# A transformer block in one kernel: when the second feed-forward products load residuals, join kept sums and fetch their chunks

## The chip, the core and the metric

The kernel runs on one core of one Trainium2 chip. The metric is device time in microseconds (us), as the median of the runs shown. One further execution was taken with the hardware profiler; its page and trace are read below. Engines are called PE (TensorE, matmuls), PEld (its weight loads), DVE (VectorE), ACT (ScalarE), POOL (GpSimd) and SP (SyncE, which here issues nearly all DMAs). L1509 is line 1509 of the kernel.

## The reference, cut to what matters

One layer over 2048 latent tokens of width 1024: token mixing (attention and a gated MLP), then the channel part. Only the last lines matter here:

```
h2 = modulate(x, norm2_g, sh2, sc2)
x = x + g2 * sq_relu_mlp(h2, w_ff1, w_ff2)     # square(relu(h2 @ w_ff1)) @ w_ff2
```

x on the right is the residual (2048 x 1024), g2 a row of 1024 factors, w_ff1 is 1024 x 4096 and w_ff2 4096 x 1024. Everything is fp32.

## The kernel before, in words

**Arithmetic.** Every fp32 operand is split into a high part h, rounded to the type that PE multiplies, and a remainder l, also in that type. A product is three matmuls: h by h (L1418), h by l (L1419), l by h (L1420), all added in one PSUM bank. The large products are cut into two by two blocks, and seven block products are formed instead of eight (a Strassen scheme); some sums of products are kept aside and used in two results.

**Feed-forward.** ffn (L1594) handles the tokens in two blocks of 1024. For each block ff1 (L1479) makes the activations in 16 groups and writes, ready for the second products, seven combined operands to DRAM (ao_d), as ff1_group does at L1446 to L1476. The weights w_ff2, combined in the same way, lie in wo_d (w2o_d in the trace), written once during the first ff1. Then ff2 (L1513) forms the second products of the block. So ff2(0), ff1(1) and ff2(1) follow each other at the end of the kernel.

**ff2.** It takes the products in the order 0, 1, 5, 6, 4, 2, 3 (L1563), each in eight chunks of 256 rows of the inner dimension: 56 steps (L1566). A chunk is 512 KB of ao_d and 512 KB of wo_d. ff2_chunk (L1502) loads each with one DMA on SP (L1507), rounds it on ACT (L1508, 128 x 1024 at a time) and subtracts on DVE for the remainder (L1509). A chunk takes four buffers of the tag b4, which has 12. Loads are made two chunks ahead: step n emits the load of chunk n + 2 (L1568). A step has four groups of six matmuls, one group per 128 tokens, each group in its own PSUM bank (128 x 512).

At the end of a product (step with c = 7) take (L1544) handles the four banks:
- products 0, 5, 6: ACT copies the bank to an f2 buffer, as kept sum u2 (0, then 5) or u3 (6) (L1548, L1555);
- product 1: the result leaves, then ACT copies the kept u2 back into the bank (L1551), on which product 5 goes on;
- products 4, 2: DVE adds the kept sum and the bank (L1558), and the result leaves; 2 goes on in the banks of 4, so in 2 the kept sum is u2 with the earlier parts in PSUM;
- product 3: the result leaves.

leave (L1535) multiplies by g2 on DVE, adds the residual xs on DVE, and puts the store to the output on a list (late, L1542). The traces give the line of the small helper, L1521, for all these DVE operations. The list is worked off in the next step, after the loads of that step (L1569). residual (L1526) loads the four xs tiles (256 KB each, L1530); it is called in the last chunk of products 1, 4, 2 and 3 (L1578). xs, kept sums, results and the side work's tiles all come from the tag f2, which has 16 buffers of 128 x 512.

**Side work.** In every step of ff2(0) one piece of side work is emitted (L1587): first the row g2 (mod_part, 12 steps, L321), then h_ops (L1328), which prepares the operands of ff1(1) in four rounds of five steps: load and scale x (L1267), transposes on PE and copies out on ACT (L1282, L1289), sums, and splits into high part and remainder (L1255, L1263 and L1264). Those operands fill all 35 buffers of the tag hb until ff1(1) ends; its products run in the order 0, 5, 1, 6, 4, 3, 2, and hb holds the operands of 6, 4, 3, 2 and a part of 1. hb is free during ff2(1).

**Order.** The tile framework sets semaphores and places each engine's instructions by a plan of its own; the sequence in the code is its priority, not its result. order (L1689) ties first writes to tiles of one tag to the code's sequence, and holds SP to it within ff2 (self.loads, L1592, L1704). ACT, DVE and PE are free to be reordered by the plan. At run time each engine works its queue strictly in that order.

Of the kernel before, what the change touches and what calls it, by code (L numbers as in the profile page):

```python
# [11 lines left out]
F32R = mybir.dt.float32r  # L12
I32 = mybir.dt.int32
AF = mybir.ActivationFunctionType
ALU = mybir.AluOpType
# [4 lines left out]
P = 128  # L20
# [10 lines left out]
TB = 512  # L31
NB = SEQ // TB
TT = TB // P
# [11 lines left out]
NCH = NG // 2  # L45
# [6 lines left out]
def f32(ap):  # L52
    return ap.bitcast(F32)
# [17 lines left out]
class Kern:  # L71
# [1427 lines left out]
            for _ in more:  # L1499
                pass  # L1500

    def ff2_chunk(self, blk, p, c):  # L1502
        nc = self.nc
        out = []
        for src in (self.ao_d[blk][p][c], self.wo_d[p][c]):
            l, h = self.sb("b4", [2, TB], F32R), self.sb("b4", [2, TB], F32R)
            nc.sync.dma_start(f32(l), src.rearrange("s p c -> p s c"))  # L1507
            nc.scalar.copy(h, f32(l))  # L1508
            nc.vector.tensor_tensor(out=l, in0=f32(l), in1=f32(h), op=ALU.subtract)  # L1509
            out.append((h, l))  # L1510
        return out

    def ff2(self, blk, side):  # L1513
        nc = self.nc
        add, mult = ALU.add, ALU.mult
        ready = self.ready + [self.ff2_chunk(blk, 0, 1)]
        begin = self.here()
        late = []

        def tt(out, in0, in1, op):  # L1520
            nc.vector.tensor_tensor(out=out, in0=in0, in1=in1, op=op)  # L1521

        goes = {1: (0, 0), 4: (1, 1), 2: (0, 1), 3: (1, 0)}
        u2, u3, xs = ([None] * TT for _ in range(3))

        def residual(p):  # L1526
            i, j = goes[p]
            for t in range(TT):
                xs[t] = self.sb("f2", [TB])
                nc.sync.dma_start(  # L1530
                    xs[t],
                    self.x1_d[2 * blk + i][t * P : (t + 1) * P, j * TB : (j + 1) * TB],
                )

        def leave(p, t, src):  # L1535
            i, j = goes[p]
            row = (2 * blk + i) * TB + t * P
            cs = slice(j * TB, (j + 1) * TB)
            c = self.sb("f2", [TB])
            tt(c, src, self.g2b[:, cs], mult)  # L1540
            tt(c, c, xs[t], add)
            late.append(lambda: nc.sync.dma_start(self.out[0, row : row + P, cs], c))  # L1542

        def take(p, t):  # L1544
            ps = banks[p][t]
            if p == 0:
                u2[t] = self.sb("f2", [TB])
                nc.scalar.copy(u2[t], ps)  # L1548
            elif p == 1:
                leave(p, t, ps)  # L1550
                nc.scalar.copy(ps, u2[t])  # L1551
            elif p in (5, 6):
                u = u2 if p == 5 else u3
                u[t] = self.sb("f2", [TB])
                nc.scalar.copy(u[t], ps)  # L1555
            elif p in (4, 2):
                u = u3[t] if p == 4 else u2[t]
                tt(u, u, ps, add)  # L1558
                leave(p, t, u)
            else:  # L1560
                leave(p, t, ps)

        order = (0, 1, 5, 6, 4, 2, 3)  # L1563
        steps = [(p, c) for p in order for c in range(NCH)]
        banks = {}
        for n, (p, c) in enumerate(steps):  # L1566
            if n + 2 < len(steps):
                ready.append(self.ff2_chunk(blk, *steps[n + 2]))  # L1568
            for f in late:  # L1569
                f()  # L1570
            late.clear()
            (ah, al), (wh, wl) = ready.pop(0)
            fresh = p in (0, 4)
            if c == 0 and fresh:
                new = [self.bank([TB]) for _ in range(TT)]
                for other in (0, 1, 5, 6, 3) if p == 0 else (4, 2):
                    banks[other] = new
            if c == NCH - 1 and p in goes:  # L1578
                residual(p)
            for t in range(TT):  # L1580
                tok = slice(t * P, (t + 1) * P)
                a = [(ah[:, s, tok], al[:, s, tok]) for s in range(2)]
                b = [(wh[:, s], wl[:, s]) for s in range(2)]
                self.product(banks[p][t], a, b, fresh and c == 0)
                if c == NCH - 1:
                    take(p, t)
            next(side, None)  # L1587
        for f in late:
            f()
        for _ in side:  # L1590
            pass
        self.loads.append(range(begin, self.here()))  # L1592

    def ffn(self, h, w, w1, late):  # L1594
        for _ in w1:
            pass
        next(late)
        next(late)
        self.ff1(0, h, self.w2_ops, w, late)
        self.g2b = self.sb("g1", [D])  # L1600
        h = self.operand_lists()
        side = chain(self.mod_part(lambda: self.sb("f2", [TB]), ("g2",)), self.h_ops(1, h))
        self.ff2(0, side)
        self.ff1(1, h, lambda g: iter(()))
        self.ff2(1, iter(()))
# [449 lines left out]
```

## Time and profile before

| | |
|---|---|
| runs | 3120.96, 3128.94, 3130.93 us; median 3128.94 |
| profiled execution, first to last instruction (span) | 3128.1 us; the page gives no other time of it |
| PE busy | 3011.9 us, 96% |
| PEld, DVE, ACT, POOL busy | 2261.8, 2070.7, 1459.0, 688.3 us |
| chain that ended last, PE's share | 79%; DMA 8%, DVE 6%, ACT 3% |
| mean granted clock of PE | 0.982 |
| ff2(0), ff1(1), ff2(1) | from about 2167, 2499 and 2807 us of the span |

How to read the lines below. A group line has: line, engine, operation, out<-in by tile names without buffer numbers, shapes, xcount, then busy us, mean ns of one, idle us of the engine just before them and who ended it. A timeline line has start us, duration us, engine, line, what, and in brackets the idle time before and its releaser. A wait line has who waited, for whom, total us, times, longest us. Durations of neighbouring matmuls overlap, since they are pipelined; their pace is read from their starts. In tile names b is the tag b4, f is f2 (or f8, f9), g is the row g2.

### The profile page before, as it was taken

How to read it: one execution, taken by the hardware profiler on the slowest of the kernel's cores; microseconds unless marked ns; L12 is line 12 of the kernel's file. 1: busy time of each engine (PE TensorE's matmuls, PEld its weight loads, DVE VectorE, ACT ScalarE, POOL GpSimd, SP SyncE). 2: the span in 40 equal slices, each digit the busy share in tenths (PEclk: the TensorE clock that was granted, in tenths of full speed). 3: DMA queues.
4: the chain of work that ended last, by engine and by line, in shares of the span. 5: the costliest groups of instructions: out<-in, count | busy, mean ns of one | idle time of the engine just before them, and what ended most of it. 6: DMA issues, size and time to landing. Idle time of an engine off the chain costs nothing.

```text
span 3128.1 us, 37962 instructions
## 1 busy us (share of the span) xinstructions
PE 3011.9 (96%) x13508; PEld 2261.8 (72%) x13508; DVE 2070.7 (66%) x2930; ACT 1459.0 (47%) x2290; POOL 688.3 (22%) x506
## 2 busy tenths in 40 slices
PE   7799999988999999999989989999999999999999
PEld 3778788866555555555867878888777788888777
DVE  3767477875887767767664478876665576654445
ACT  4545765563555554545222245444454354444433
POOL 0000000000888888886144200000000000000000
PEclk9899999999999999999999999999999999999999
DMA  7586657654001000004864448888766644445665
GB/s 260 169 271 216 209 188 226 198 170 145 27 31 38 12 7 18 11 8 159 271 217 158 138 150 314 307 301 289 247 218 220 207 144 155 154 161 194 205 214 202
DMA packets 389807, 534.33 MB, mean 171 GB/s; under 512 B 37968, under 2 KB 209104, under 8 KB 389616
## 3 DMA queue, kind: packets, MB, share of 16 engines
q1 hardware_dynamic: 374720, 515.88, 49.7%
q10 hardware_dynamic: 14896, 16.02, 1.5%
q8 instruction: 106, 1.74, 0.2%
q14 instruction: 85, 0.70, 0.1%
HBM read 367.69 MB, written 164.10 MB: 170 GB/s over the span
## 4 chain that ended last, share of the span: by engine, by line
PE 79%; DMA 8%; DVE 6%; ACT 3%; issue 2%; POOL 1%; SPq 1%; ACTq 0%; DVEq 0%; POOLq 0%
PE b L1419 13%; PE b L1420 13%; PE b L1418 13%; PE b L1947 8%; PE b L1914 5%; PE b L1933 4%; PE b L183 4%; PE b L185 4%; PE b L184 4%; PE b L1879 3%; PE a L1418 2%; PE a L1419 2%; PE a L1420 2%; PE b L189 2%; DMA f<-in_w_in 1%
## 5 line engine op out<-in xcount | busy, mean ns | idle before, releaser
L1509 DVE TENSOR_TENSOR b<-b,b 128x1024 fp32r<-128x1024 f32 x224 | 273.0, 1224 | 246.4 <-ACT b L1508 241.8
L1890 DVE TENSOR_REDUCE ts<-b 128x1 f32<-128x512 f32 x512 | 314.9, 682 | 142.2 <-PE b L1879 142.0
L1508 ACT CAST b<-b 128x1024 fp32r<-128x1024 f32 x224 | 234.9, 1052 | 332.5 <-DMA b<-ao_d 298.1
L1419 PE MATMUL b<-b,b 128*128 128x512 f32 x896 | 351.6, 392 | 4.1 <-DVE b L1509 3.5
L1420 PE MATMUL b<-b,b 128*128 128x512 f32 x896 | 349.7, 390 | 0.0
L1418 PE MATMUL b<-b,b 128*128 128x512 f32 x896 | 309.0, 395 | 12.4 <-ACT b L1508 7.6
L1963 POOL TENSOR_TENSOR ac<-ac,p 128x512 f32<-128x512 f32 x216 | 302.2, 1433 | 67.8 <-ACT p L1937 67.2
L1937 ACT ACTIVATE p<-b 128x512 f32<-128x512 f32 x384 | 199.8, 614 | 167.0 <-PE b L1933 157.1
L1963 POOL TENSOR_TENSOR ac<-ac,t 128x512 f32<-128x512 f32 x152 | 217.8, 1460 | 0.0
L1418 PEld LDWEIGHTS b<-b,b 128*128 128x128 f32 x896 | 168.4, 189 | 54.7 <-ACT b L1508 11.9
L1914 PE MATMUL b<-h,h 128*128 128x512 f32 x576 | 200.9, 419 | 1.8 <-DVE ts L1890 1.2
L1419 PEld LDWEIGHTS b<-b,b 128*128 128x128 f32 x896 | 168.9, 188 | 45.4 <-DVE b L1509 10.7
L1420 PEld LDWEIGHTS b<-b,b 128*128 128x128 f32 x896 | 168.7, 188 | 34.6
L1933 PE MATMUL b<-h,h 128*128 128x512 f32 x576 | 180.7, 395 | 0.0
L1947 PE MATMUL b<-p,h 128*64 128x512 f32 x768 | 175.3, 598 | 0.0
L1419 PE MATMUL b<-hb,b 128*128 128x512 f32 x448 | 174.6, 390 | 0.0
L1836 POOL MEMSET t<- 128x512 f32 x16 | 8.4, 527 | 723.0 <-DMA tb_d<-t 699.5
L1418 PE MATMUL b<-hb,b 128*128 128x512 f32 x416 | 162.1, 390 | 0.0
L1420 PE MATMUL b<-hb,b 128*128 128x512 f32 x416 | 161.5, 389 | 0.0
L1428 DVE TENSOR_TENSOR f<-f,b 128x512 f32<-128x512 f32 x160 | 109.3, 683 | 65.9 <-issue 43.2
L1914 PEld LDWEIGHTS b<-h,h 128*128 128x128 f32 x576 | 107.0, 190 | 59.3 <-DVE ts L1890 20.1
L1418 PE MATMUL a<-f,h 128*128 128x384 f32 (+1 forms) x320 | 119.3, 376 | 14.5 <-ACT a L608 8.5
(393 smaller groups left out, 6920.0 us busy)
## 6 DMA issues: line engine op xcount, KB each, us to landing
ao_d<-f SPq DMA_DIRECT2D x224, 256.0 KB
b<-ao_d SPq DMA_DIRECT2D x112, 512.0 KB
b<-w2o_d SPq DMA_DIRECT2D x112, 512.0 KB
f<-in_w_ff SPq DMA_DIRECT2D x48, 1024.0 KB
w2o_d<-f SPq DMA_DIRECT2D x112, 256.0 KB
f<-in_w_in SPq DMA_DIRECT2D x46, 512.0 KB
f<-x_d SPq DMA_DIRECT2D x64, 256.0 KB
m<-p_d SPq DMA_DIRECT2D x20, 512.0 KB
```

What stands on the lines that cost most here:

```text
L183: mm(ps, sh, mh, start=start, stop=False)
L1418: mm(ps, wh, hh, start=start and k == 0, stop=False, skip_group_check=True)
L1419: mm(ps, wh, hl, start=False, stop=False, skip_group_check=True)
L1420: mm(ps, wl, hh, start=False, stop=k == len(w) - 1, skip_group_check=True)
L1508: nc.scalar.copy(h, f32(l))
L1509: nc.vector.tensor_tensor(out=l, in0=f32(l), in1=f32(h), op=ALU.subtract)
L1890: nc.vector.tensor_reduce(out=self.mx[:, t, h, c : c + 1], in_=ps[h], axis=AX.X, op=ALU.max)
L1914: self.nc.tensor.matmul(self.pts[j][h], k.KA[c][self.kv][:, ks], self.qa[h], start=True, stop=False, skip_group_check=True,)
L1933: self.nc.tensor.matmul(s, k.KB[c][self.kv][:, ks], self.qb[h], start=False, stop=True, skip_group_check=True,)
L1937: self.nc.scalar.activation(pt[h], s, AF.Exp)
L1947: nc.tensor.matmul(self.o[h * HD : (h + 1) * HD, :], k.V[c][:, i, self.kv * HD : (self.kv + 1) * HD], pt[h], start=j == 0, stop=j == NKT - 1,)
L1963: nc.gpsimd.tensor_tensor(out=self.acc[e][:, h], in0=old[:, h], in1=pt[h], op=ALU.add)
```

## The change

It touches ff2_chunk, ff2 and one line of ffn.

1. Residuals (xs) are loaded in chunk 5 of products 1, 4, 2, 3 instead of chunk 7.
2. For products 4 and 2 the kept sum is joined to the residual beforehand: carried, emitted in chunk 6, multiplies the kept sum by g2 and adds it to xs. At the end of the product only the bank is multiplied by g2 there.
3. leave emits only the multiplication. The addition of xs is put on the list with the store, and so is emitted in the next step, after the loads of that step.
4. In ff2(1) chunks are fetched four ahead instead of two. Odd chunks are loaded there in four pieces of 256 KB into hb buffers (eight per chunk), with four casts and four subtractions of 128 x 512; even chunks as before into b4.
5. In ff2(0) two empty steps stand between mod_part and h_ops, so that h_ops starts two chunks later.

```
-    def ff2_chunk(self, blk, p, c):
+    def ff2_chunk(self, blk, p, c, apart=False):
...
         for src in (self.ao_d[blk][p][c], self.wo_d[p][c]):
+            if apart:
+                pairs = []
+                for s in range(2):
+                    l, h = self.sb("hb", [TB], F32R), self.sb("hb", [TB], F32R)
+                    nc.sync.dma_start(f32(l), src[s])
+                    nc.scalar.copy(h, f32(l))
+                    nc.vector.tensor_tensor(out=l, in0=f32(l), in1=f32(h), op=ALU.subtract)
+                    pairs.append((h, l))
+                out.append(pairs)
+                continue
...
-        ready = self.ready + [self.ff2_chunk(blk, 0, 1)]
+        ahead = 4 if blk else 2
+        def chunk(n):
+            return self.ff2_chunk(blk, *steps[n], bool(blk) and n % 2 == 1)
+        ready = self.ready + [chunk(n) for n in range(1, ahead)]
...
+        def carried(p):
+            _, cs = place(p)
+            for t in range(TT):
+                u = (u3 if p == 4 else u2)[t]
+                tt(u, u, self.g2b[:, cs], mult)
+                tt(xs[t], xs[t], u, add)
...
         def leave(p, t, src):
...
+            c, x = self.sb("f2", [TB]), xs[t]
             tt(c, src, self.g2b[:, cs], mult)
-            tt(c, c, xs[t], add)
-            late.append(lambda: nc.sync.dma_start(self.out[0, row : row + P, cs], c))
+            def rest():
+                tt(c, c, x, add)
+                lo = row + t * P
+                nc.sync.dma_start(self.out[0, lo : lo + P, cs], c)
+            late.append(rest)
...
-            elif p in (4, 2):
-                u = u3[t] if p == 4 else u2[t]
-                tt(u, u, ps, add)
-                leave(p, t, u)
...
-            if n + 2 < len(steps):
-                ready.append(self.ff2_chunk(blk, *steps[n + 2]))
+            if n + ahead < len(steps):
+                ready.append(chunk(n + ahead))
...
-            if c == NCH - 1 and p in goes:
+            if c == NCH - 3 and p in goes:
                 residual(p)
+            if c == NCH - 2 and p in (4, 2):
+                carried(p)
...
-        side = chain(self.mod_part(lambda: self.sb("f2", [TB]), ("g2",)), self.h_ops(1, h))
+        side = chain(
+            self.mod_part(lambda: self.sb("f2", [TB]), ("g2",)), [None] * 2, self.h_ops(1, h)
+        )
```

More of the change, by code (lines that the diff above doesn't have):

```diff
@@ L1509, in ff2_chunk @@
             nc.vector.tensor_tensor(out=l, in0=f32(l), in1=f32(h), op=ALU.subtract)
-            out.append((h, l))
+            out.append([(h[:, s], l[:, s]) for s in range(2)])
         return out
@@ L1515, in ff2 @@
         add, mult = ALU.add, ALU.mult
-        ready = self.ready + [self.ff2_chunk(blk, 0, 1)]
+        order = (0, 1, 5, 6, 4, 2, 3)
+        steps = [(p, c) for p in order for c in range(NCH)]
+        ahead = 4 if blk else 2
+        def chunk(n):
+            return self.ff2_chunk(blk, *steps[n], bool(blk) and n % 2 == 1)
+        ready = self.ready + [chunk(n) for n in range(1, ahead)]
         begin = self.here()
@@ L1524, in ff2, with place @@
         u2, u3, xs = ([None] * TT for _ in range(3))
+        def place(p):
+            i, j = goes[p]
+            return (2 * blk + i) * TB, slice(j * TB, (j + 1) * TB)
         def residual(p):
@@ L1533, in residual @@
                 )
+        def carried(p):
[4 more added lines that the diff above has]
+                tt(xs[t], xs[t], u, add)
         def leave(p, t, src):
[L1536 to L1539, printed above, removed]
+            row, cs = place(p)
+            c, x = self.sb("f2", [TB]), xs[t]
             tt(c, src, self.g2b[:, cs], mult)
-            tt(c, c, xs[t], add)
-            late.append(lambda: nc.sync.dma_start(self.out[0, row : row + P, cs], c))
+            def rest():
[3 more added lines that the diff above has]
+            late.append(rest)
         def take(p, t):
             ps = banks[p][t]
[L1546 to L1553, printed above, removed]
+            if p in (0, 5, 6):
+                u = u3 if p == 6 else u2
                 u[t] = self.sb("f2", [TB])
                 nc.scalar.copy(u[t], ps)
-            elif p in (4, 2):
-                u = u3[t] if p == 4 else u2[t]
-                tt(u, u, ps, add)
-                leave(p, t, u)
             else:
                 leave(p, t, ps)
-        order = (0, 1, 5, 6, 4, 2, 3)
-        steps = [(p, c) for p in order for c in range(NCH)]
+                if p == 1:
+                    nc.scalar.copy(ps, u2[t])
         banks = {}
         for n, (p, c) in enumerate(steps):
-            if n + 2 < len(steps):
-                ready.append(self.ff2_chunk(blk, *steps[n + 2]))
+            if n + ahead < len(steps):
+                ready.append(chunk(n + ahead))
             for f in late:
@@ L1571, in ff2 @@
             late.clear()
-            (ah, al), (wh, wl) = ready.pop(0)
+            a, b = ready.pop(0)
             fresh = p in (0, 4)
@@ L1577, in ff2 @@
                     banks[other] = new
-            if c == NCH - 1 and p in goes:
+            if c == NCH - 3 and p in goes:
                 residual(p)
+            if c == NCH - 2 and p in (4, 2):
+                carried(p)
             for t in range(TT):
                 tok = slice(t * P, (t + 1) * P)
-                a = [(ah[:, s, tok], al[:, s, tok]) for s in range(2)]
-                b = [(wh[:, s], wl[:, s]) for s in range(2)]
-                self.product(banks[p][t], a, b, fresh and c == 0)
+                at = [tuple(x[:, tok] for x in pair) for pair in a]
+                self.product(banks[p][t], at, b, fresh and c == 0)
                 if c == NCH - 1:
```

## The prediction, made before the changed kernel was run

> **What bounds the kernel now.** I read the page first, then busy time by window for the two runs of second products, then the chain for the pace of the matmuls, then who waited for whom, and last the order of time around the waits.
>
> ```profile
> span 3128.1 us, 37962 instructions
> ```
> ```profile
> 2167.00:2499.00 332.00, 322.07 (x1416) 260.94 (x1415) 203.76 (x218) 148.58 (x173) 0.00 (x0) 0.99 0.69 229
> 2807.00:3123.00 316.00, 309.30 (x1346) 251.16 (x1344) 156.07 (x151) 122.29 (x127) 0.00 (x0) 1.00 0.61 206
> ```
> ```profile
> 3101.15 0.91 PE b L1418 x4
> 3106.59 0.91 PE b L1418 x4
> ```
> ```profile
> L189 PE MATMUL b<-ident,f 128*128 128x128 f32 x64 | 7.6, 272 | 0.0
> ```
>
> The two windows run from the first to the last matmul of ff2(0) and ff2(1). Their columns are length, busy time of PE, PEld, DVE, ACT and POOL, granted clock, DMA share and GB/s. TensorE (PE) is the bound: apart from its own weight loads no engine is busy for two thirds of either window. The two chain rows are the starts of neighbouring chunks: 24 matmuls take 5.44 us, 0.227 us each. 56 chunks take 304.6 us at that pace. So ff2(1) stands 316.0 - 304.6 = 11.4 us above its floor; ff2(0) stands 27.4 above, of which the 64 transposes of the next block's operands are 7.6, so under 20 are left, with a few foreign matmuls in them. No edit to ff2 can gain much more than 11 + 18 = 29 us, 0.9% of the span. Who made PE wait, first in ff2(0), then in ff2(1) (total, times, longest):
>
> ```profile
> PE b L1418 <- ACT b L1508: 5.4, 6, 2.4
> PE b L1418 <- ACT b L1551: 2.2, 1, 2.2
> PE b L1419 <- DVE b L1509: 1.9, 3, 1.0
> ```
> ```profile
> PE b L1418 <- ACT b L1551: 2.4, 2, 1.7
> PE b L1418 <- ACT b L1508: 2.2, 4, 0.8
> PE b L1419 <- DVE b L1509: 1.7, 2, 1.0
> ```
>
> PE never waits for a transfer itself, but for the cast (L1508), the remainder (L1509) or a bank refilled by a copy (L1551). Idle time is 9.5 and 6.3 us; the rest of the loss is slow pace after a wait. The two longest waits:
>
> ```profile
> 2261.57 0.80 PE L1418 MATMUL b<-b,b 128*128 128x512 f32 x1 [2.25 <-ACT b L1551]
> ```
> ```profile
> 2262.00:2264.50 2.50, 2.50 (x7) 1.91 (x7) 2.50 (x6) 1.18 (x2) 0.00 (x0) 0.50 0.85 306
> ```
> ```profile
> 2350.47 1.65 PE L1418 MATMUL b<-b,b 128*128 128x512 f32 x3 [2.39 <-ACT b L1508]
> ```
>
> After 2.25 us of idleness the granted clock is 0.50 for the next 2.5 us: about 2 us more are lost, so such a wait costs 4.2 to 4.4 us in all, not 2.3. The Trainium skill (TensorE: Matmul & The Clock Gate, Part 1) lets the clock fall after an idle window of about 3.4 us; by that rule alone these two would cost 4.6 us together instead of 8.6, and the 2.5 us that I give to (b) of ff2(0) below would be 1.4. The measured 0.50 decides here.
>
> **Why the waits are there.** Three kinds, each with one place of ff2(1).
>
> (a) An in-order engine stands at an operation that waits for PE, with the next chunk's operands queued behind it. End of product 0, ACT:
>
> ```profile
> 2849.77 0.59 ACT L1548 COPY f<-b 128x512 f32<-128x512 f32 x1 [0.54 <-PE b L1420]
> 2850.25 1.05 ACT L1508 CAST b<-b 128x1024 fp32r<-128x1024 f32 x1
> ```
>
> The cast of the next chunk comes after the third of four copies that keep the sums. End of product 4, DVE:
>
> ```profile
> 3031.51 0.69 DVE L1521 TENSOR_TENSOR f<-f,b 128x512 f32<-128x512 f32 x1 [0.38 <-PE b L1420]
> 3032.11 2.35 DVE L1509 TENSOR_TENSOR b<-b,b 128x1024 fp32r<-128x1024 f32 x2
> ```
>
> The remainder comes after the last addition that reads PSUM. Costs of single places I take from the starts of neighbouring matmuls, as what each step has over 0.227 us. By them each such place costs 1.1 to 1.3 us; ff2(1) has five (ends of 0, 5, 6, 4, 2): 5.9 us, with 0.3 us of aftermath.
>
> (b) The other way round, at the end of product 1:
>
> ```profile
> 2894.68 1.23 DVE L1509 TENSOR_TENSOR b<-b,b 128x1024 fp32r<-128x1024 f32 x1 [2.79 <-ACT b L1508]
> 2895.83 0.68 DVE L1521 TENSOR_TENSOR f<-b,g 128x512 f32<-128x512 f32 x1
> ```
>
> The first multiplication, which frees a bank, stands behind the remainder of a chunk whose data had only just come; then additions stand between the multiplications. Cost 3.1 us in ff2(1), 4.2 in ff2(0).
>
> (c) SP stops. Its order in ff2 is that of the code:
>
> ```profile
> 3071.92 1.90 SPq L1530 DMA_DIRECT2D f<-x_d  x4
> 3076.43 0.37 SPq L1507 DMA_DIRECT2D b<-ao_d  x1
> 3076.91 0.41 SPq L1507 DMA_DIRECT2D b<-w2o_d  x1
> 3081.99 5.08 SPq L1542 DMA_DIRECT2D out_x<-f  x4
> 3087.16 0.39 SPq L1507 DMA_DIRECT2D b<-ao_d  x1
> ```
> ```profile
> SPq L1507 <- PE b L1420: 197.2, 44, 4.9
> SPq L1542 <- DVE f L1521: 35.1, 16, 10.4
> ```
>
> The stores wait for additions, and the chunk load that could have gone one chunk (5.44 us) after 3076.4 goes at 3087.2: 1.4 us of stall a chunk later. With the 0.7 us at the seam to ff1 the list for ff2(1) is 5.9 + 0.3 + 3.1 + 1.4 + 0.7 = 11.4, the whole excess. In ff2(0) the same kinds meet the side work; its worst is a load for ff1 that SP holds until a buffer is free:
>
> ```profile
> 2336.75 1.65 SPq L1507 DMA_DIRECT2D b<-w2o_d  x1
> 2346.96 0.37 SPq L1359 DMA_DIRECT2D f<-in_w_ff  x1
> 2347.38 0.58 SPq L1507 DMA_DIRECT2D b<-ao_d  x1
> ```
>
> That is the 4.4 us at 2350. ff2(0) by kind: (b) 4.2; transposes and this load 1.4 + 1.8 + 4.4; (a) four times 1.1 to 1.3; (c) 1.3; together 17.9.
>
> **The change part by part.**
>
> *Four chunks ahead in ff2(1).* SP's 197 us of waiting for PE are waits for a free b4 buffer (12 hold three chunks). With odd chunks in hb (35 hold four) a load needs no buffer younger than two chunks, so it goes about five chunks ahead. That is 27 us of lead for what (c) delays by 10.4. Casts and remainders of a chunk can then run well before the end of a product; (a), (b) and (c) lose their cause together, 10.7 us. I take 10. The lower end is 4.5, (b) and (c) alone, if the queues of ACT and DVE keep their order; the upper 10.7.
>
> Its cost: 28 odd chunks with four casts and four remainders of 128x512 instead of two of 128x1024.
>
> ```profile
> L1509 DVE TENSOR_TENSOR b<-b,b 128x1024 fp32r<-128x1024 f32 x108 | 131.7, 1225 | 145.4 <-ACT b L1508 142.5
> L1508 ACT CAST b<-b 128x1024 fp32r<-128x1024 f32 x107 | 112.2, 1053 | 170.6 <-DMA b<-ao_d 158.6 <-DMA b<-w2o_d 11.2 <-PE b L1419 0.8
> ```
> ```profile
> L1263 ACT CAST hb<-f 128x512 fp32r<-128x512 f32 x17 | 9.8, 620 | 2.9 <-DVE f L1345 2.7
> ```
> ```profile
> L1264 DVE TENSOR_TENSOR hb<-f,hb 128x512 fp32r<-128x512 f32 x17 | 11.0, 685 | 0.0
> ```
>
> ACT: 28 x (4 x 0.620 - 2 x 1.053) = 10 us; DVE: 28 x (4 x 0.685 - 2 x 1.225) = 8 us. Both engines are under half busy in that window; PE's 304.6 us hide it. SP issues two more loads per odd chunk, by the four residual issues 0.47 us each: 0.9 us per 10.9, against 197 us of waiting. Costed at nothing; without cover it would be at most these 10 us.
>
> At the start, chunk 1 needs eight hb buffers that hold ff1's operands until its last products; ff1 ends 0.4 us before 2807.2 and chunk 1 is due at 2812.6. Eleven of them are free before the last three products, 36 matmuls or 8 us before the end. That is 13 us before they are due; a load that followed the four of the residual (3076.4 above) was cast 5.2 us after its issue, and casts and remainders add some 4:
>
> ```profile
> 3081.66 2.22 ACT L1508 CAST b<-b 128x1024 fp32r<-128x1024 f32 x2 [4.46 <-DMA b<-ao_d]
> ```
>
> Were they the last ones to come free, about 3 us would be lost. I take 0.3, range 0 to 3.
>
> *Residual at chunk 5, kept sums joined at chunk 6.* The four loads are only moved. Products 4 and 2 change from three operations per 128 rows to four:
>
> ```profile
> L1521 DVE TENSOR_TENSOR f<-f,f 128x512 f32<-128x512 f32 x16 | 10.6, 686 | 0.1
> ```
>
> That is 8 x 0.686 = 5.5 us of DVE more per block, beside matmuls; but after the last matmul of a product only one operation per 128 rows waits for PE, where there were three. In chunk 6 DVE has 8 x 0.686 + 2.45 = 7.9 us for 5.44; the 2.5 us over are gone by chunk 0 of the next product. With two chunks ahead that eats a slack of about 3 us; I count nothing, range 0 to 2 twice in ff2(0).
>
> *Additions one chunk on.* After product 1 DVE does four multiplications without additions between: (b) in ff2(0) loses perhaps 2.5 of 4.2, for the first multiplication can still stand behind a remainder. (c) in ff2(0): stores follow sooner after the last matmul, since eight operations instead of twelve stand before them, 2.7 us off a stop of about 5: its 1.3 us go. Gain 3.8 in ff2(0); (a) there keeps its cause, the operation on PSUM ahead of the remainder, so I take nothing from it.
>
> *Side work two steps later.* At the end of product 1 the kept sums (4), the residual (4), the results (4) and eight tiles of a round of side work wanted 20 of f2's 16 buffers; two steps later the round's second four come after the kept sums are gone, and 16 do. The four rounds fall on other chunks; their 7.6 us may become 2 or 12. No row says which: counted unchanged, range -5 to +5.
>
> *The end.* Now:
>
> ```profile
> 3122.21 1.43 DVE L1521 TENSOR_TENSOR f<-b,g 128x512 f32<-128x512 f32 x2
> 3123.56 1.28 DVE L1521 TENSOR_TENSOR f<-f,f 128x512 f32<-128x512 f32 x2
> ```
> ```profile
> 3121.00 4.21 SPq L1542 DMA_DIRECT2D out_x<-f  x4
> ```
>
> Two additions follow the last multiplication, each with its store. If all four do, 2 x 0.69 = 1.4 us are added; I take half, 0.7.
>
> **Sum:** 3128.1 - 10 - 3.8 + 0.3 + 0.7 = 3115.3 us for the span. The page has no other time of that execution; the median of the runs shown, 3128.94, is 0.8 above it, so I forecast 3116.
>
> **The rivals.**
>
> *Orders stay (0.25).* The loads go out earlier, but ACT and DVE keep the copies and PSUM reads ahead of the next operands. For it: at every chunk start four L1418 come in a row, so the plan expects the remainder late throughout. Against it: the loads of two tags no longer hang on one chain of buffers. Only (b) and (c) of ff2(1), 4.5, and about 3 of ff2(0) go, the end adds 1: 3128.1 - 6.5 + 0.8 = 3122.
>
> *All of it goes (0.07).* ff2(0) loses its rounds' stalls too: 3128.1 - 27 + 0.8 = 3102. Against it: nothing in the change loads further ahead there.
>
> *Small loads bind (0.06), slower.* In ff2(1) DMA share is 0.61 for 64 MB, 56 of them chunks; odd chunks are 0.27 of it. If a 256 KB load costs f times as much per byte, the share over the floor of 304.6 us is 0.35 + 0.28 f; from f = 2.3 loads are the bound. At f = 2.7 ff2(1) takes 304.6 x 1.10 = 335 us, 19 more: 3128.1 + 19 - 3.8 + 1 = 3144. Against it: the load behind the four 256 KB ones of the residual still reached its cast in 5.2 us, and DMA reached 306 GB/s in the row above amid such loads. The Trainium skill (DMA: Bandwidth & Descriptors, Rules for kernel authors) asks for 1 MiB and more per DMA, which speaks against this split; an estimate from its sizes, 64 KB in 0.95 and 1 MB in 6.15 us, (Bandwidth, Measured), is f = 1.2, under the bound.
>
> **How the numbers follow.** Forecast 0.62, own range 3110 to 3121 (10 between 4.5 and 10.7, rounds +-5). Faster or slower by 0.3% is 9.4 us, about what a measurement of this kernel can tell from no change; faster means below 3119.5. Forecast: 0.56 faster, 0.05 same, 0.01 slower; orders stay: 0.25 same; all goes: 0.07 faster; small loads: 0.06 slower. Range 3106 to 3127: it leaves out small loads, all goes and few ends of the forecast.
>
> **What would show it.** Right: ff2(1) in 305 to 307 us with no PE wait over 0.5 us, chunk loads on SP some five chunks before use. Wrong: PE waiting for casts or remainders at the ends of products in ff2(1) (orders stay); DMA share near 1 there (small loads); several 2 us waits in ff2(0) (rounds); DVE's last four additions all after the last multiplication and the end over 7 us after the last matmul.

## The result, and the profile after

The change made no difference that can be measured. Medians of twelve runs each are 3128.82 us after and 3129.32 us before; the estimated ratio after to before is 1.0002, with a 95% interval of 0.9991 to 1.0012, so even its sign is open. Forecast was 3116, range 3106 to 3127.

The profile shows that two differences cancel. Busy time by window, from first to last matmul of ff2(0) and of ff2(1), kernel after (columns as above):

```profile
2165.00:2504.00 339.00, 325.08 (x1414) 261.80 (x1413) 207.77 (x225) 148.32 (x173) 0.00 (x0) 0.98 0.67 224
2812.00:3123.00 311.00, 307.18 (x1348) 252.13 (x1346) 157.23 (x211) 123.77 (x181) 0.00 (x0) 1.00 0.60 208
```

ff2(0) took 339 us instead of 332, ff2(1) 311 instead of 316. More exactly, I call the time from the start of a stage's first matmul to the start of its last one its length, and the time from there to the end of the span the end. (The lengths of ff2(0) stop two matmuls early, 0.45 us, in every row alike; this changes no difference.)

| kernel | ff2(0) | ff2(1) | end |
|---|---|---|---|
| floor (1343 x 0.2267 us) | 304.4 | 304.4 | |
| before | 331.35 | 315.34 | 5.62 |
| before, once more (e1) | 332.37 | 315.83 | 5.61 |
| after | 338.72 | 309.86 | 7.01 |

ff2(0) lost 6.4 to 7.4 us, ff2(1) gained 5.5 to 6.0, the end lost 1.4: in all 1.8 to 3.3 us more, inside the interval. Who made PE wait, kernel after, in ff2(0) and in ff2(1):

```profile
PE b L1419 <- DVE b L1519: 6.8, 8, 2.3
PE b L1418 <- ACT b L1518: 5.6, 7, 2.3
PE b L1418 <- ACT b L1584: 0.6, 1, 0.6
PE b L1418 <- DVE f L1538: 0.4, 1, 0.4
```
```profile
PE b L1418 <- ACT b L1518: 3.5, 3, 1.6
```

L1518 and L1519 are now the cast and the remainder. In ff2(1) only three waits are left, all for casts. In ff2(0) waiting for remainders went from 1.9 to 6.8 us.

Where the losses of PE lie shows more than totals. The table sums, for the first chunk after the end of a product, where its cost appears, what the steps between matmuls had over their pace (us). Where a group of 16 transposes of the side work lies among them, 1.8 us are taken off, which such a group takes elsewhere:

| kernel, stage | after end of 0 | of 1 | of 5 | of 6 | of 4 | of 2 |
|---|---|---|---|---|---|---|
| before, ff2(1) | 1.1 | 3.2 | 1.1 | 1.1 | 1.4 | 1.4 |
| after, ff2(1) | 0.9 | 0.0 | 2.3 | 2.3 | 0.0 | 0.0 |
| before, ff2(0) | 0.0 | 4.3 | 1.1 | 1.1 | 1.4 | 1.4 |
| after, ff2(0) | 0.0 | 4.5 | 1.4 | 3.0 | 2.6 | 4.2 |

**ff2(1): the lead was there, and thrown away.** ACT around the end of product 5, kernel after:

```profile
2942.45 1.56 ACT L1580 COPY f<-b 128x512 f32<-128x512 f32 x3 [20.82 <-PE b L1420]
2944.26 0.58 ACT L1580 COPY f<-b 128x512 f32<-128x512 f32 x1 [0.25 <-PE b L1420]
2944.74 1.05 ACT L1518 CAST b<-b 128x1024 fp32r<-128x1024 f32 x1
2945.69 2.18 ACT L1511 CAST hb<-hb 128x512 fp32r<-128x512 f32 x4
2947.77 2.00 ACT L1518 CAST b<-b 128x1024 fp32r<-128x1024 f32 x2
```

ACT stood 20.8 us at the first copy, which waits for PE, with the casts of nearly four chunks queued behind it. Then it did them in a burst, in which these casts did not wait for a load, and PE waited 1.62 us for the first of them:

```profile
2945.84 0.96 PE L1418 MATMUL b<-b,b 128*128 128x512 f32 x3 [1.62 <-ACT b L1518]
```

**ff2(0): the remainder comes later.** After the end of product 2, PE and DVE, kernel after:

```profile
2459.47 0.61 PE L1419 MATMUL b<-b,b 128*128 128x512 f32 x1 [2.28 <-DVE b L1519]
```
```profile
2456.40 1.28 DVE L1538 TENSOR_TENSOR f<-b,g 128x512 f32<-128x512 f32 x2
2457.60 0.68 DVE L1538 TENSOR_TENSOR f<-f,f 128x512 f32<-128x512 f32 x1
2458.20 1.22 DVE L1519 TENSOR_TENSOR b<-b,b 128x1024 fp32r<-128x1024 f32 x1
```

An addition of the residual (f<-f,f), which nobody waits for, stands ahead of the remainder that PE waits for; another stood ahead of the remainder at 2455.27. In the kernel before, no multiplication and no addition of the residual stood ahead of the remainders there:

```profile
2453.34 2.35 DVE L1509 TENSOR_TENSOR b<-b,b 128x1024 fp32r<-128x1024 f32 x2
2455.61 0.69 DVE L1521 TENSOR_TENSOR f<-f,g 128x512 f32<-128x512 f32 x1
```

### The profile page after: what moved, and what is told of

Read it like the earlier page. It is cut to its first block, busy times and chain, and to the rows that moved or that the text cites. A ratio compares the mean times of both kernels' runs of the same rounds, so it can differ in the third digit from the quotient of the medians.

```text
span 3129.5 us, 38096 instructions
## 1 busy us (share of the span) xinstructions
PE 3007.5 (96%) x13508; PEld 2257.9 (72%) x13508; DVE 2078.1 (66%) x3002; ACT 1459.8 (47%) x2346; POOL 687.2 (22%) x506
## 5 line engine op out<-in xcount | busy, mean ns | idle before, releaser
L1519 DVE TENSOR_TENSOR b<-b,b 128x1024 fp32r<-128x1024 f32 x168 | 202.7, 1221 | 140.5 <-ACT b L1518 138.7
L1518 ACT CAST b<-b 128x1024 fp32r<-128x1024 f32 x168 | 175.4, 1051 | 217.5 <-DMA b<-ao_d 181.5
L1419 PE MATMUL b<-b,b 128*128 128x512 f32 x672 | 265.6, 395 | 7.2 <-DVE b L1519 6.8
L1420 PE MATMUL b<-b,b 128*128 128x512 f32 x672 | 263.9, 393 | 0.0
L1418 PE MATMUL b<-b,b 128*128 128x512 f32 x672 | 232.3, 395 | 10.4 <-ACT b L1518 9.2
L1418 PEld LDWEIGHTS b<-b,b 128*128 128x128 f32 x672 | 126.2, 189 | 43.1 <-ACT b L1518 13.4
L1419 PEld LDWEIGHTS b<-b,b 128*128 128x128 f32 x672 | 127.4, 190 | 39.3 <-DVE b L1519 13.0
L1428 DVE TENSOR_TENSOR f<-f,b 128x512 f32<-128x512 f32 x160 | 109.0, 681 | 57.1 <-issue 41.8
L1420 PEld LDWEIGHTS b<-b,b 128*128 128x128 f32 x672 | 127.5, 190 | 26.2
```

The costliest lines, as they stand in the source:

```text
L1418: mm(ps, wh, hh, start=start and k == 0, stop=False, skip_group_check=True)
L1419: mm(ps, wh, hl, start=False, stop=False, skip_group_check=True)
L1420: mm(ps, wl, hh, start=False, stop=k == len(w) - 1, skip_group_check=True)
```

## The experiments

The theory (A): the parts of the change are harmless in themselves; what counts is the order that the framework's plan gives to ACT, DVE and PE, and each part shifts that order. In ff2(1) it wastes the lead; in ff2(0) one of the parts puts work ahead of remainders. The rivals are named with each run.

All kernels are the changed one with its parts behind constants, one value for ff2(0) and one for ff2(1); its lines stand 8 further down in what is shown (L1426 to L1428 the matmuls, L1526 cast, L1527 remainder, L1546 the helper's DVE operations). HELD names engines that are kept to the code's sequence in a block, by the same means as SP's:

```
 RESIDUAL = (5, 5)          # chunk in which the residual is loaded        (part 1)
 JOIN = (True, True)        # kept sums joined to it beforehand            (part 2)
 MOVED = (True, True)       # additions one chunk on                       (part 3)
 AHEAD = (2, 4)             # chunks loaded ahead                          (part 4)
 SHIFT = 2                  # empty steps ahead of h_ops                   (part 5)
 HELD = ((), ())
 LAST_AT_ONCE = False       # product 3 of ff2(1): additions not put off
...
+        kept = {(n, getattr(self.nc, e).engine) for r, es in self.kept for n in r for e in es}
...
+            held = held or (idx, i.engine) in kept
```

Results, all from profiles; the ratio to the kernel before with its 95% interval where a kernel ran more than once. Three chips were used, one for e1 to e4, one for e5 to e8, one for e9 to e12:

| run | ff2(0) | ff2(1) | end | ratio |
|---|---|---|---|---|
| e2_ahead_only | 332.91 | 312.44 | 6.82 | 0.9994 (0.9982 to 1.0006) |
| e3_held | 340.36 | 306.26 | 6.99 | 0.9981 (0.9967 to 0.9994) |
| e4_best | 333.18 | 305.55 | 7.23 | 0.9972 (0.9962 to 0.9983) |
| e5_pe_held | 332.39 | 305.71 | 5.06 | 0.9958 (0.9942 to 0.9974) |
| e6_no_shift | 336.01 | 309.85 | 6.99 | |
| e7_no_join | 337.40 | 309.88 | 7.00 | |
| e8_shift_only | 330.11 | 316.58 | 5.62 | |
| e9_final | 327.99 | 306.37 | 5.06 | 0.9950 (0.9934 to 0.9965) |
| e10_residual_early | 340.19 | 305.40 | 5.06 | |
| e11_moved | 331.57 | 306.06 | 5.06 | |
| e12_all_held | 344.75 | 305.47 | 5.05 | 0.9994 (0.9983 to 1.0006) |

**e1_before_again**: no edit.

> The kernel before once more. Length of a stage means from the start of its first matmul to the start of its last one. In the two profiles so far ff2(0) took 331.35 us before and 338.72 after, ff2(1) 315.34 and 309.86, the end after the last matmul 5.62 and 7.01. If stage lengths are set by the order of the program, this run repeats 331.4, 315.3 and 5.6 within 0.5 us each, even if the whole time differs by several us. If they scatter by several us from run to run, the comparison by stage means little and only the timed rounds count.

332.37, 315.83 and 5.61: ff2(0) was 1.0 off, a little more than expected, the others within 0.5. Over all runs with ff2(0) as before (before, e1, e2, e4, e5) it took 331.4 to 333.2. So a length can be read to about 2 us from one profile, and a smaller difference between two profiles shows nothing by itself.

**e2_ahead_only**:

```
-RESIDUAL = (5, 5)
-JOIN = (True, True)
-MOVED = (True, True)
-SHIFT = 2
+RESIDUAL = (7, 7)
+JOIN = (False, False)
+MOVED = (False, False)
+SHIFT = 0
```

> Only part 4 of the change: in ff2(1) four chunks ahead with odd chunks in hb; residual, kept sums, additions and side work as before. Theory A (the parts act in the blocks in which they stand, and the four-ahead loads are what gained 5.5 us in ff2(1)): ff2(0) 331.4, ff2(1) 309 to 311, end 5.6, in all 5 us less than before, ratio 0.998. Rival B (the gain in ff2(1) is that of the moved additions, and the lead brings nothing): ff2(1) 313 to 316, ratio 1.000.

312.44: between the two, so both had a part. The lead alone brought 3 us; parts 1 to 3 in ff2(1) brought another 2.6 (309.9). What they took away there are 2.4 us after each of the ends of 4 and 2, where in e2 three DVE operations for each bank still stood; 2.3 us after the end of 5, where e2 loses nothing, came in their place. The end of 6.82 us, with additions untouched, contradicts both: put-off additions aren't what lengthened it.

**e3_held**:

```
-HELD = ((), ())
+HELD = ((), ("scalar", "vector"))
```

> The changed kernel with ACT and DVE held to the sequence of the code within ff2(1), as SP already is. Theory A (the lead of four chunks is lost because the plan puts the copies and multiplications at the end of a product ahead of the casts of up to four following chunks, so that ACT stands for 15 to 21 us at a copy with landed data behind it): ff2(1) 305 to 307 us, no wait of PE over 0.5 us inside it; ff2(0) stays at 338.7. Rival B (the casts and remainders come in time, but too many of them meet at a product's end: ACT or DVE throughput, or the loads, set the wait): ff2(1) stays at 309 to 311.

306.26, as theory A says, with one wait over 0.5 us left (1.56 us at a bank after the end of product 4). ACT at the end of product 5, run e3:

```profile
2943.92 0.59 ACT L1593 COPY f<-b 128x512 f32<-128x512 f32 x1 [0.77 <-PE b L1428]
2945.28 0.59 ACT L1593 COPY f<-b 128x512 f32<-128x512 f32 x1 [0.77 <-PE b L1428]
2945.76 2.00 ACT L1526 CAST b<-b 128x1024 fp32r<-128x1024 f32 x2
```

The copies still wait for PE, but what follows them is a chunk that is due in 20 us, and PE does not wait. ACT and DVE do the same operations as in the kernel after, so their throughput did not set the wait.

**e4_best**:

```
-RESIDUAL = (5, 5)
-JOIN = (True, True)
-MOVED = (True, True)
-SHIFT = 2
-HELD = ((), ())
-LAST_AT_ONCE = False
+RESIDUAL = (7, 5)
+JOIN = (False, True)
+MOVED = (False, True)
+SHIFT = 0
+HELD = ((), ("scalar", "vector"))
+LAST_AT_ONCE = True
```

> ff2(0) as before in everything; in ff2(1) the change, with ACT and DVE held to the code's sequence, and the additions of the last product not put off. Theory A: ff2(0) 331.4, ff2(1) 305 to 307, end 5.6: 9 to 10 us less than before, about 3119, ratio 0.997. Rival B: ff2(1) 309 to 311, 5 us less, ratio 0.998. If ff2(0) is not back at 331.4, what is done in ff2(1) reaches back into ff2(0).

ff2(0) returned to 333, ff2(1) was 305.55; 0.28% less than before. Only the end missed: 7.23 us, though each addition followed its multiplication.

**e5_pe_held** (to e4):

```
-HELD = ((), ("scalar", "vector"))
+HELD = ((), ("scalar", "vector", "tensor"))
```

> e4_best with PE too held to the code's sequence within ff2(1), so that each group of 128 tokens gets its six matmuls together. Theory A (the end after the last matmul grew from 5.6 to 7.0 us in every run with split chunks, not because additions were put off, but because the plan takes the first half of a split chunk for all four banks before the second half, so the first bank is complete 1.4 instead of 3.0 us before the last matmul): end 5.6 to 5.8, ff2(1) 305 to 306, in all 1.5 us less than e4_best. Rival B (the end is set by DVE's eight operations and the stores): end stays at 7.0 to 7.2. ff2(0) 331 to 333.

The end fell to 5.06 us, below that of the kernel before. First DVE operation of the end in e2, and in e5, beside the start of the last matmul:

```profile
3122.45 1.29 DVE L1546 TENSOR_TENSOR f<-b,g 128x512 f32<-128x512 f32 x2 [15.29 <-PE b L1428]
```
```profile
3123.83 0.39 PE L1428 MATMUL b<-hb,hb 128*128 128x512 f32 x1
```
```profile
3111.00 0.69 DVE L1546 TENSOR_TENSOR f<-b,g 128x512 f32<-128x512 f32 x1 [19.32 <-PE b L1428]
```
```profile
3114.66 0.39 PE L1428 MATMUL b<-hb,hb 128*128 128x512 f32 x1
```

In e2 the first bank is ready 1.4 us before the last matmul starts, in e5 3.7: with a split chunk the plan had PE go through all four banks with the first half, and only then with the second. So five of the eight DVE operations start after the last matmul has started, in e5 two, in the kernel before three.

**e6_no_shift** (to the change):

```
-SHIFT = 2
+SHIFT = 0
```

> The changed kernel without part 5, the two empty steps. Theory A (ff2(0) lost 7 us chiefly because the four rounds of side work fall on other chunks, two of them on the ends of products 5 and 6): ff2(0) 333 to 335 instead of 338.7 to 340.4. Rival B (it lost by the joined sums and moved additions at the ends of products 4 and 2): ff2(0) 338 to 340. ff2(1) as after, 309 to 311, by both.

336.0: of the loss of 6 to 7 us at most 3 to 4 go with part 5, and 4.2 us each stay after the ends of 4 and 2. Both ranges missed; neither theory holds as put.

**e7_no_join** (to the change):

```
-JOIN = (True, True)
+JOIN = (False, True)
```

> The changed kernel with the kept sums of products 4 and 2 added in ff2(0) as before, at the product's end; additions of the residual still one chunk on, two empty steps kept. Theory A (side work): ff2(0) 338 to 340. Rival B (the eight more operations and the order they bring at the ends of 4 and 2): ff2(0) 335 to 337, with the waits at the ends of 4 and 2 back at 1.3 us each.

337.4, just outside both ranges, with 2.8 and 4.3 us after the ends of 4 and 2. Joining is not the main cause.

**e8_shift_only** (to the kernel before):

```
-SHIFT = 0
+SHIFT = 2
```

> The kernel before with part 5 alone, the two empty steps. Theory A (side work): ff2(0) 335 to 337, against 331.4 to 333.2 without them. Rival B: ff2(0) 331 to 333. ff2(1) as before, 315 to 316, by both.

330.1, below both ranges. Theory A on the side work fell: part 5 by itself does no harm. After the end of product 1 the loss is 1.3 us, where in the five runs with ff2(0) as before it was 3.5 to 4.6. PE there:

```profile
2261.09 1.97 PE L197 MATMUL b<-ident,f 128*128 128x128 f32 x16
2263.75 0.50 PE L1426 MATMUL b<-b,b 128*128 128x512 f32 x1 [0.70 <-ACT b L1601]
```

The bank comes no sooner: from the last matmul of product 1 to the first of product 5 there are 3.2 us, in the kernel before 2.6. But a group of transposes, which elsewhere takes 1.8 us of its own, now falls into that time. So, of the parts that act in ff2(0), the loss came from part 1 or 3, the only ones common to e6 and e7 and absent here.

**e9_final** (to e5):

```
-SHIFT = 0
+SHIFT = 2
```

> ff2(0) with part 5 alone (as e8_shift_only), ff2(1) as e5_pe_held. Theory A (the two blocks act apart, and part 5 by itself gains 1 to 2 us in ff2(0)): ff2(0) 330 to 331, ff2(1) 305.5 to 306, end 5.1: some 12 us less than before, ratio 0.996 or a little under. Rival B (330.1 in e8_shift_only was scatter): ff2(0) 331.5 to 333.5, as e5_pe_held.

ff2(0) 328.0, less than forecast and less than in e8; ff2(1) 306.4, a little more. Both runs with part 5 alone lie below all five without it, so part 5 gains. This version is faster than the kernel before: ratio 0.9950 (0.9934 to 0.9965), an interval that also lies below that of the changed kernel.

**e10_residual_early** and **e11_moved** (each to e9):

```
-RESIDUAL = (7, 5)
+RESIDUAL = (5, 5)
```
```
-MOVED = (False, True)
+MOVED = (True, True)
```

> e9_final with one thing more in ff2(0): the residual loaded in chunk 5 instead of 7 (part 1); additions at the product's end, kept sums not joined. Theory A (part 1 did the harm in ff2(0): with the residual there early, the plan puts each addition right behind its multiplication, ahead of the next chunk's remainder, which it otherwise leaves until the residual comes): ff2(0) 334 to 338, with 2.5 to 4.3 us lost at each of the ends of products 4 and 2 instead of 1.3. Rival B (part 3, the moved additions, did it): ff2(0) as in e9_final, 330 to 333.

> e9_final with one thing more in ff2(0): the additions of the residual emitted one chunk later (part 3); residual still loaded in chunk 7, kept sums not joined. Theory A (part 1 did the harm): ff2(0) 330 to 333, losses at the ends of 4 and 2 1.3 us each. Rival B (part 3 did it): 334 to 338, 2.5 to 4.3 us at each of these ends.

The early residual alone took ff2(0) from 328.0 to 340.2 us, more than theory A had said; the moved additions alone left it at 331.6, 1.5 and 3.6 above the two runs without them (e8, e9). After the ends of 1, 4 and 2 e10 loses 4.5, 5.2 and 4.8 us, e11 1.3 each time, as e9 does within 0.1. DVE after the end of product 2, e9:

```profile
2449.61 0.69 DVE L1546 TENSOR_TENSOR f<-f,b 128x512 f32<-128x512 f32 x1 [5.54 <-PE b L1428]
2450.22 1.22 DVE L1527 TENSOR_TENSOR b<-b,b 128x1024 fp32r<-128x1024 f32 x1
2451.35 1.28 DVE L1546 TENSOR_TENSOR f<-f,b 128x512 f32<-128x512 f32 x2
2453.01 0.69 DVE L1546 TENSOR_TENSOR f<-f,b 128x512 f32<-128x512 f32 x1 [0.38 <-PE b L1428]
2453.62 2.35 DVE L1527 TENSOR_TENSOR b<-b,b 128x1024 fp32r<-128x1024 f32 x2
2455.89 0.69 DVE L1546 TENSOR_TENSOR f<-f,g 128x512 f32<-128x512 f32 x1
2456.49 1.22 DVE L1527 TENSOR_TENSOR b<-b,b 128x1024 fp32r<-128x1024 f32 x1
2457.63 0.69 DVE L1546 TENSOR_TENSOR f<-f,f 128x512 f32<-128x512 f32 x1
```

and e10:

```profile
2459.65 0.69 DVE L1546 TENSOR_TENSOR f<-f,b 128x512 f32<-128x512 f32 x1 [5.54 <-PE b L1428]
2460.37 0.69 DVE L1546 TENSOR_TENSOR f<-f,g 128x512 f32<-128x512 f32 x1
2460.98 0.68 DVE L1546 TENSOR_TENSOR f<-f,b 128x512 f32<-128x512 f32 x1
2461.58 0.69 DVE L1546 TENSOR_TENSOR f<-f,f 128x512 f32<-128x512 f32 x1
2462.18 1.22 DVE L1527 TENSOR_TENSOR b<-b,b 128x1024 fp32r<-128x1024 f32 x1
...
2465.71 1.23 DVE L1527 TENSOR_TENSOR b<-b,b 128x1024 fp32r<-128x1024 f32 x1
```

The operations are the same. In e9 multiplications (f<-f,g) and additions (f<-f,f) come after the two remainders that PE needs next (2450.22 and the first at 2453.62); in e10, where the residual is loaded two chunks earlier, the plan puts three multiplications and two additions ahead of the second. That remainder starts 6.1 us after the first operation on PSUM instead of 4.0. It did not wait for data, since its cast in e10 had ended at 2459.5:

```profile
2458.45 1.05 ACT L1526 CAST b<-b 128x1024 fp32r<-128x1024 f32 x1 [0.23 <-DMA b<-w2o_d]
```

PE pays:

```profile
2454.89 0.50 PE L1427 MATMUL b<-b,b 128*128 128x512 f32 x1 [1.01 <-DVE b L1527]
```
```profile
2466.99 0.80 PE L1427 MATMUL b<-b,b 128*128 128x512 f32 x1 [3.08 <-DVE b L1527]
```

first e9, then e10: 2.1 us more of idleness, and in the 2.5 us that follow a granted clock of 0.50, in e9 1.00. At the end of product 1 the early residual turned ACT's order round too. First e9, where the casts of the next product's first chunk come before the bank is refilled (L1601), then e10, where they stand behind it:

```profile
2253.05 1.05 ACT L1526 CAST b<-b 128x1024 fp32r<-128x1024 f32 x1 [0.35 <-DMA b<-w2o_d]
2260.92 0.59 ACT L1601 COPY b<-f 128x512 f32<-128x512 f32 x1 [0.54 <-DVE f L1546]
```
```profile
2258.37 0.59 ACT L1601 COPY b<-f 128x512 f32<-128x512 f32 x1 [7.65 <-DVE f L1546]
2258.89 1.05 ACT L1526 CAST b<-b 128x1024 fp32r<-128x1024 f32 x1
```

The late residual had kept both orders right by accident. Why the multiplications move too is not shown: they do not read the residual, but order ties the first write of their f2 tiles to come after that of the residual's.

**e12_all_held** (to the change):

```
-HELD = ((), ())
-LAST_AT_ONCE = False
+HELD = (("scalar", "vector", "tensor"), ("scalar", "vector", "tensor"))
+LAST_AT_ONCE = True
```

> The change in full in both blocks, with ACT, DVE and PE held to the code's sequence in ff2(0) too (and the last product's additions not put off). Theory A (the change is sound as it is written, and only the plan's order spoils it): ff2(0) under 330, the ends of products 1, 4 and 2 under 1.3 us each, ff2(1) 305.5 to 306. Rival B (the side work of ff2(0) needs the plan: in the sequence of the code its transposes, copies and splits stand in PE's, ACT's and DVE's way): ff2(0) over 335.

344.75 in ff2(0): the number of rival B. The longest waits of PE there, of 6.1 us for a cast and 3.3 us for transposes (L197) behind the scaling of x (L1287):

```profile
PE b L1426 <- ACT b L1526: 10.0, 3, 6.1
PE b L197 <- DVE f L1287: 3.3, 1, 3.3
```

The reason that rival B gives covers only a part. The two largest losses, 8.3 us at the start of product 2 and 7.5 us in chunk 3 of product 3, lie where the side work has ended: with the two empty steps it takes the first 34 of the 56, and product 2 starts at step 41. In chunk 3 of product 3 a load came late, since SP had stood some 9 us before four stores:

```profile
2475.61 1.04 ACT L1526 CAST b<-b 128x1024 fp32r<-128x1024 f32 x1 [10.00 <-DMA b<-ao_d]
```

So the code's sequence is no cure in itself: it is good in ff2(1), which has no side work and data about five chunks early, and bad in ff2(0), which has neither advantage. No run separates the two.

## Why the prediction was wrong, point by point

- **The step that failed: "The four loads are only moved ... I count nothing, range 0 to 2 twice in ff2(0)."** I asked when the data would land and what DVE would have to do, but not what the late residual did to the order of DVE and ACT. It held back operations that could wait. Loading it early, and nothing else, costs 12 us beside part 5 (340.2 in e10 against 328.0 in e9). The parts do not add up: the whole change took about as long as e10 (338.7, and 340.4 in e3), and without part 5 it took 336.0 (e6). Against the kernel before the loss was 6.4 to 7.4 us, where I forecast a gain of 3.8. No rival held this. "Orders stay" had the outcome "same", at 3122, but counted a gain of 3 us in ff2(0); that a gain and a loss cancelled would have been luck for it.
- **Four chunks ahead, 10 us: mechanism right, size wrong.** 5.5 to 6.0 us came, and the lead by itself brought only about 3 of them (e2); the rest came with parts 1 to 3. (b) and (c) and the ends of 4 and 2 went, as forecast; the ends of 0, 5 and 6 stayed, at 0.9, 2.3 and 2.3 us. That the lead is there before the end of a product I had right; that the casts "can then run well before" it was the mistake, since the plan had copies ahead of them. My rival "orders stay" named this, but for all five ends. With the order held (e3, e4), and parts 1 to 3 in place, 9 to 10 us came.
- **(a) in ff2(0), nothing:** 1.2 and 2.8 us more lost after the ends of 4 and 2, by the failed step. The 3.0 after the end of 6 came with part 5: e9 loses as much there, e6 1.4. **(b) in ff2(0), 2.5 us gained:** nothing gained, 4.5 lost where it was 4.3, by the failed step. **(c) in ff2(0), 1.3:** right in size, since product 3 lost nothing there after its first chunk, but by luck: with the moved additions alone 1.0 us stays (e11), with the early residual alone none (e10).
- **Side work, counted unchanged, -5 to +5:** by itself it gained: 330.1 and 328.0 against 331.4 to 333.2 (e8, e9); beside the early residual it cost 2.7 to 4.4 us (e6 against the two runs of the change in ff2(0)). After the end of product 1 the gain was 2 to 3 us, but not shown to be by the count of f2 buffers that I gave: the bank came no sooner, transposes filled the wait.
- **The end, 0.7:** 1.4, and for another reason: not the put-off additions but PE's order in a split chunk (e2, e5).
- **Split loads, casts and remainders at no cost, start 0.3:** right. ff2(1) came to 305.4 with them (e10), 1 us above its floor, and lost nothing in product 0; DMA share was 0.60 in the kernel after, 0.61 before. The rival "small loads bind" fell: 256 KB loads among those of 512 KB kept up at 208 GB/s. The Trainium skill (DMA: Bandwidth & Descriptors, Rules for kernel authors) advises 1 MiB or more per DMA for full bandwidth; at this rate, in this stage, that was not needed.
- **The pool of 11 us in ff2(1)** was the right bound: 10 of them could be had.

## What to carry to other kernels

When a list scheduler orders the engines, moving a load earlier also removes a wait that its order depended on: look at what was sorted behind that wait, and ask who it will now stand in front of. Fetching further ahead helps only if the operations that turn a load into an operand are not queued behind something that waits for the bound engine; look for long idle times of ACT or DVE before a copy, with landed data behind it. And test a change made for two unlike stages in each stage apart: here ff2(1) gained by parts that cost time in ff2(0).

## What the runs showed of the hardware

The clock of PE fell to half after shorter waits than I had taken, and did not fall after longer ones. Kernel after, granted clock 0.50, 1.00 and 0.50 (the column before DMA share) right behind three places:

```profile
2258.50:2261.50 3.00, 3.00 (x9) 2.32 (x8) 3.00 (x3) 0.00 (x0) 0.00 (x0) 0.50 1.03 364
2361.70:2364.20 2.50, 2.45 (x10) 1.69 (x11) 2.50 (x4) 1.90 (x4) 0.00 (x0) 1.00 1.01 357
2372.00:2374.20 2.20, 2.20 (x6) 1.72 (x6) 2.20 (x4) 1.96 (x2) 0.00 (x0) 0.50 0.03 10
```
```profile
2361.64 1.21 PE L1418 MATMUL b<-b,b 128*128 128x512 f32 x4 [2.32 <-ACT b L1518]
```

The second follows a single wait of 2.32 us and kept full clock. The first follows three waits of 0.46, 0.60 and 0.62 us within 3 us, the third one of 1.70 us three microseconds behind one of 0.56. So neither the longest single wait nor the sum of the waits decides: 2.32 us in one piece kept full clock, 1.7 us in three pieces did not. Nor does a wait of 2.25 us always cost the half clock that the prediction counted with it. In e1, the kernel before once more, the same wait at the same place left the clock at 1.00:

```profile
2254.84 0.50 PE L1426 MATMUL b<-b,b 128*128 128x512 f32 x1 [2.26 <-ACT b L1601]
```
```profile
2255.30:2257.80 2.50, 1.84 (x9) 1.18 (x8) 2.50 (x5) 1.25 (x3) 0.00 (x0) 1.00 0.83 319
```

What decides stays open. The Trainium skill (TensorE: Matmul & The Clock Gate, Part 1) has a free-running window of about 3.4 us that must be idle before the clock falls; here it fell after waits of at most 1.70 us, so this trace does not agree.

The scatter of the whole time lies elsewhere: the first matmul of ff1(0), up to which the code is the same in all kernels, started between 1843.0 us (e1) and 1853.6 us (e8) of the span, while ff2(1) of the kernel before took 315.3 and 315.8 us. What scatters before that point is open.
